# SwiGLU of an fp32 hybrid decoder: the second product of two token tiles in seven block products, its operands split and stored by the first product

## The chip, the cores and the metric

The kernel runs on one core of a Trainium2 chip. The metric is the device time of one execution in microseconds. Smaller is better.

## What is computed

One inference step of a decoder with two layers, on 1024 prompt tokens and 32 sample tokens (8 sequences of 4), with 1024 channels. Layer 0 mixes tokens by windowed attention, layer 1 by a gated linear recurrence, and each layer ends with the same gated feed-forward block, which is where most of the work lies:

```
def swiglu(h, w_in, w_out):
    g, u = jnp.split(h @ w_in, 2, axis=-1)
    return (jax.nn.silu(g) * u) @ w_out

for layer in range(DEPTH):                      # DEPTH = 2
    ...                                         # attention or recurrence
    xp = xp + swiglu(rms_norm(xp, ffn_norm[layer]), w_ffn_in[layer], w_ffn_out[layer])
    xs = xs + swiglu(rms_norm(xs, ffn_norm[layer]), w_ffn_in[layer], w_ffn_out[layer])
```

The hidden width is 2816, that is 22 blocks of 128, so `h @ w_in` is a product with 1024 x 5632 and the second one with 2816 x 1024. Everything is float32.

## The kernel before

**Data and precision.** Channels lie on the partitions, tokens along the free axis. The 1056 tokens are three tiles, t = 0 and 1 with 384 columns, t = 2 with 288 (256 prompt tokens and the 32 sample tokens). A float32 product is made from three matmuls in the faster fp32r format: every operand is split into a high part (a copy to fp32r, on ACT) and a low part (the value minus the high part, on DVE), and `mm3` (L244) issues high times high, high times low and low times high into one PSUM bank. So a block product of 128 x 128 with 384 columns is three matmuls on PE.

**Phases.** Attention lasts to about 390 us of the span, the first feed-forward block to about 1121, the recurrence to about 1458, the second feed-forward block to the end. Each feed-forward block (`ffn_phase`) has two halves.

**First product.** For each hidden block f, the gate and the up weights are loaded (`Weight`: one DMA of 512 KB, a copy on ACT, L83, a subtraction on DVE, L87). Blocks 0 and 1 are plain: `h_in` runs 48 matmuls for each tile. For f = 2 to 21 tiles 0 and 1 together are a 2 x 2 block problem (two tiles by two halves of the 1024 input channels, gate and up beside each other) that `seven` solves with seven block products in place of eight, in Strassen's manner: 84 matmuls of 384 columns, where the plain form has 96. The sums of inputs that it needs are formed once per layer (`sums`, `sum4`), those of weights once per f on DVE (`Sums`, L110 to L116). Tile 2 stays plain (48 matmuls of 288). Hidden values go to DRAM (`store`, L801, 192 KB for a block of 384 columns).

**Second product.** `outs` goes over 11 chunks of two hidden blocks each, and in a chunk over the three tiles. `Hidden` loads the stored values back and splits them (ACT L282, DVE L283). `h_out` takes, for each of the 8 output blocks m, one PSUM bank and 6 matmuls, and DVE adds the bank to the running x (L923). Per chunk that is 96 matmuls of 384 columns and 48 of 288. Nothing is waited for in a chunk but the DVE add eight banks back: there are 8 PSUM banks and each is used once.

**What sets the order.** PE and the DMA queue of SP run in the order in which the code issues. ACT, DVE and POOL are put in order by the scheduler of the language, at build time: the order of their instructions is fixed in the program, and each engine takes them strictly one after the other, so an instruction that waits holds all behind it. `drive` (L220) walks over the list of items; before an item runs, whatever it needs is prepared, and after it as many further preparations as slots are free for. There are 6 slots for split weights, 2 buffers `raw` for what has just been loaded, 18 slots of activations and 6 more ("h").

**Scores of the attention.** `att_rounds` computes the scores of a unit (four heads, 128 queries) from two halves of the partitions, 64 channels each. For each half one bank is taken, and for each of two heads one `mm3`: 6 matmuls of 64 partitions in the one half, then 6 in the other.

Of the kernel before, what the change touches and what calls it, by code (L numbers as in the profile page):

```python
# [29 lines left out]
NT = 3  # L30
# [25 lines left out]
class Slots:  # L56
    def __init__(self, names):
        self.free = list(names)
# [84 lines left out]


class Item:
    def __init__(self, fn, needs=(), frees=None):
        self.fn, self.needs = fn, list(needs)
        self.frees = self.needs if frees is None else list(frees)
        self.halves = [self]
# [36 lines left out]
class Kern:  # L186
# [33 lines left out]
    def drive(self, items):  # L220
        need = [w for it in items if isinstance(it, Item) for w in it.needs]
# [263 lines left out]
    def att_rounds(self, t):  # L485
# [5 lines left out]
        def scores(u):  # L491
# [8 lines left out]
            qc = slice(b * P, (b + 1) * P)  # L500
            jobs = []
            for hf in range(2):
                r = slice(hf * 64, hf * 64 + 64)
                ps = self.bank("s")
                for hh in range(2):
                    o = ps[:, hh * 256:hh * 256 + N]
                    self.mm3(o, q[r, hh, 0, qc], q[r, hh, 1, qc], kt[r, 0, k0:k0 + N], kt[r, 1, k0:k0 + N], True, True)
                    jobs.append((o, 8 * p + 4 * hf + 2 * hp + hh, hf * 2 + hh))
            st[u] = (jobs, nk, i, p, hp)
# [251 lines left out]
    def ffn_phase(self, l, before, after):  # L761
# [6 lines left out]
        hs = Slots([f"h{i}" for i in range(6)])  # L768
        T, HD_ = {}, {}
        late = []  # L770
        NPL = 2
        tt = nc.vector.tensor_tensor

        def enter():
# [4 lines left out]
            dp = pool("dF", space=bass.MemoryType.DRAM)  # L779
            for c in range(NF // 2):  # L780
                for t in range(NT):
                    HD_[c, t] = dp.tile([P, 2, WID[t]], F32, name=self.nm("hd"), tag=f"hd{c}_{t}")
            if l == 0:
# [16 lines left out]
        def store(f, t, src):  # L800
            late.append(lambda: nc.sync.dma_start(HD_[f // 2, t][:, f % 2, :], src))  # L801


        def h_in(wg, wu, f, t, mid=(), last=False):
# [9 lines left out]
            def post():  # L814
                sg = self.tmp([P, WMAX], "sg")
                nc.scalar.activation(sg[:, :W], g[:, :W], AF.Silu)  # L816
                tt(sg[:, :W], u[:, :W], sg[:, :W], OP.mult)  # L817
                store(f, t, sg[:, :W])

# [42 lines left out]
        def seven(wg, wu, ws, f):  # L862
            wc, wd = ws
            B11, B21, B22 = self.xn[0][:2], self.xn[0][2:], self.xn[1][2:]
            Tx = {i: [x[0] for x in T[i]] for i in T}

# [5 lines left out]

            A, B, C, Dk = self.bank(), self.bank(), self.bank(), self.bank()
            pc, u2 = small(f"e{2 * (f % 2)}"), small(f"e{2 * (f % 2) + 1}")
            prod(A, wg, 0, B11, True)
            nc.scalar.activation(pc, A[:, :WMAX], AF.Copy)
            prod(B, wd, 0, Tx[2], True)
            tt(u2, B[:, :WMAX], pc, OP.add)
            prod(C, wc, 0, Tx[3], True)
            tt(pc, C[:, :WMAX], u2, OP.add)  # L880
            prod(Dk, wc, 1, Tx[1], True)
            tt(pc, Dk[:, :WMAX], pc, OP.add)
            flush()
            prod(A, wg, 1, B21, False)
            sg = self.tmp([P, WMAX], "sg")
            nc.scalar.activation(sg, A[:, :WMAX], AF.Silu)
            prod(Dk, wd, 1, B22, False)
            g1 = self.gt.tile([P, WMAX], F32, name=self.nm("xs"), tag="xs", bufs=2)
            tt(g1, Dk[:, :WMAX], u2, OP.add)  # L889
            nc.scalar.activation(g1, g1, AF.Silu)  # L890
            prod(C, wu, 1, Tx[4], False)
            if f == NF - 1:
                self.freeall(self.xn[0] + self.xn[1][2:])
                for i in T:
                    for x, s in T[i]:
                        s.put(x[1])

            def post():
                tt(pc, pc, g1, OP.mult)
                store(f, 1, pc)  # L900
                tt(u2, C[:, :WMAX], u2, OP.add)
                tt(u2, u2, sg, OP.mult)
                store(f, 0, u2)

            return post


        def h_out(w0, w1, h, ch, t, fin, mid):
            W = WID[t]
            ws = (w0, w1)  # L910
            groups = [(m, 1) for m in range(KB)]
            if fin:
                groups = groups[4:] if l == 1 and t == 2 else [(4, 4)]
                groups = [(0, 4)] + groups
            for m0, grp in groups:
                pss = [self.bank() for _ in range(grp)]
                for c in range(2):
                    for ps, m in zip(pss, range(m0, m0 + grp)):
                        self.mm3(ps[:, :W], ws[c][:, 0, m * P:(m + 1) * P], ws[c][:, 1, m * P:(m + 1) * P],
                                 h[:, c, 0, :W], h[:, c, 1, :W], c == 0, c == 1)  # L920
                for ps, m in zip(pss, range(m0, m0 + grp)):
                    x = self.xview(t, m)
                    nc.vector.tensor_tensor(x, ps[:, :W], x, OP.add)  # L923
                    if fin and (l == 1 or t < 2):
                        self.square(t, m)
                if m0 + grp == 4:
                    for fn in mid:
                        fn()

# [12 lines left out]

        def outs(ch, fin=False, mid=((), (), ())):
            w = [Weight(I[f"wd{l}"][2 * ch + k], True) for k in range(2)]
            h = [Hidden(HD_, ch, t, hs, lambda: self.hp) for t in range(NT)]
            return [Item(lambda a, b, h, t=t: h_out(a, b, h, ch, t, fin, mid[t]), w + [h[t]],
                         (w if t == 2 else []) + [h[t]]) for t in range(NT)]

        n0, n1 = after
# [6 lines left out]
        for f in range(NPL, NF):  # L956
            L += blocks(f)
        L += [flush]
        nch = NF // 2
        for ch in range(nch - 2):  # L960
            if l == 0:
                L.append(lambda b=ch: self.caches(b) if b < DB else None)
            L += outs(ch)
        p = outs(nch - 2, False, ((), n0[1:2], n1[1:2]))
        o = outs(nch - 1, True, ((), n0[3:4], n1[3:4]))
        L += [p[0], o[0], p[1], o[1]] + n0[4:] + [p[2], o[2]] + n1[4:]
        if l == 0:
# [371 lines left out]
```

## Time and profile before

| what | value |
|---|---|
| median of three runs | 2211.83 us (2208.38 to 2214.43) |
| the profiled execution | 2209.49 us, its span 2207.7 us |
| mean granted TensorE clock | 0.994 of full speed |
| PE busy | 2167.9 us, 98% of the span |
| DVE / ACT / POOL busy | 1491.5 / 899.8 / 117.8 us |
| moved by DMA | 198.01 MB, mean 90 GB/s |

The profiled execution is 1.8 us longer than its span (what lies before the first and behind the last instruction that is counted), and 2.3 us below the median of the three runs. In the profile L12 means line 12 of the kernel; a row of a group gives the engine, the operation, out<-in by the names of the program, the shape and the count. Times are microseconds unless marked ns. PE is the matmul side of TensorE, PEld its loads of weights, DVE is VectorE, ACT is ScalarE, POOL is GpSimd.

### The profile page before, as it was taken

The numbers are of one execution on the slowest core, as the hardware profiler recorded it, in microseconds if no ns is written. First come the engines' busy times: TensorE is split into PE (matmuls) and PEld (weight loads), VectorE is DVE, ScalarE is ACT, GpSimd is POOL, SyncE is SP. The second block draws the span as 40 slices with busy tenths as digits, with TensorE's granted clock in tenths as the row PEclk, the third lists the DMA queues.
The fourth block names the chain that finished last, engine by engine and source line by source line (L and its number), as shares of the span: only waits on it lengthen the run. The fifth ranks groups of instructions, "written<-read, shape, count | busy, mean of one in ns | idle before, by whom it ended". The sixth has DMA issues, their size and how long they took to land.

```text
span 2207.7 us, 35068 instructions
## 1 busy us (share of the span) xinstructions
PE 2167.9 (98%) x13848; PEld 2145.6 (97%) x13848; DVE 1491.5 (68%) x2928; ACT 899.8 (41%) x1595; POOL 117.8 (5%) x168
## 2 busy tenths in 40 slices
PE   9999999999999999999999989999999999999997
PEld 8999999999999999999999989999999999999997
DVE  6776778855555556777786787788555555577766
ACT  5666665422223223211268887753222322321213
POOL 1223231000000000000000000000000000000002
PEclk9999999999999999999999999999999999999998
DMA  5332334212222124333212123421222212343222
GB/s 191 99 102 81 105 104 137 68 59 87 76 70 87 62 84 150 109 100 94 62 51 65 58 86 110 131 77 61 87 66 80 87 58 87 105 126 91 88 69 79
DMA packets 76045, 198.01 MB, mean 90 GB/s; under 512 B 9256, under 2 KB 32360, under 8 KB 75880
## 3 DMA queue, kind: packets, MB, share of 16 engines
q1 hardware_dynamic: 75120, 195.45, 27.7%
q8 instruction: 108, 1.77, 0.3%
q14 instruction: 57, 0.47, 0.1%
q10 hardware_dynamic: 760, 0.33, 0.1%
HBM read 167.12 MB, written 30.62 MB: 90 GB/s over the span
## 4 chain that ended last, share of the span: by engine, by line
PE 87%; DVE 7%; ACT 3%; issue 1%; DMA 1%; POOL 1%; SPq 0%; DVEq 0%; POOLq 0%; ACTq 0%
PE mm L244 82%; PE s L244 1%; DVE w L87 1%; PE pt L552 1%; DVE xs L349 1%; ACT w L83 1%; DVE xn L283 1%; DVE s L522 0%; DVE acc L300 0%; POOL x L1199 0%; DMA raw<-in_wg 0%; ACT g L1062 0%; DVE g L1110 0%; PE mm L307 0%; DVE T L283 0%
## 5 line engine op out<-in xcount | busy, mean ns | idle before, releaser
L244 PE MATMUL mm<-xn,w 128*128 128x384 f32 (+1 forms) x5808 | 929.0, 318 | 16.8 <-DVE x L687 4.6
L244 PEld LDWEIGHTS mm<-xn,w 128*128 128x128 f32 x5808 | 903.1, 189 | 23.4 <-issue 4.8
L244 PE MATMUL mm<-h,w 128*128 128x384 f32 (+1 forms) x3168 | 511.2, 322 | 1.0 <-DVE rc L311 0.6
L244 PEld LDWEIGHTS mm<-h,w 128*128 128x128 f32 x3168 | 508.8, 188 | 1.3 <-DVE rc L311 0.8
L83 ACT ACTIVATE w<-raw 128x1024 fp32r<-128x1024 f32 x248 | 262.0, 1058 | 394.8 <-PE mm L244 162.1
L87 DVE TENSOR_TENSOR w<-raw,w 128x1024 fp32r<-128x1024 f32 x246 | 300.8, 1224 | 100.4 <-ACT w L83 95.5
L244 PE MATMUL mm<-T,w 128*128 128x384 f32 x1920 | 350.9, 338 | 0.0
L923 DVE TENSOR_TENSOR x<-mm,x 128x384 f32<-128x384 f32 (+1 forms) x528 | 265.0, 521 | 116.9 <-PE mm L244 116.6
L244 PEld LDWEIGHTS mm<-T,w 128*128 128x128 f32 x1920 | 338.7, 188 | 0.0
L817 DVE TENSOR_TENSOR sg<-mm,sg 128x288 f32<-128x288 f32 (+1 forms) x52 | 24.5, 470 | 176.7 <-PE mm L244 176.6
L111 ACT ACTIVATE w<-raw 128x1024 fp32r<-128x1024 f32 x40 | 42.4, 1060 | 209.5 <-PE mm L244 207.6
L282 ACT ACTIVATE h<-raw 128x768 fp32r<-128x768 f32 (+1 forms) x66 | 52.1, 789 | 174.5 <-PE mm L244 141.8
L312 POOL TENSOR_TENSOR rc<-rc,mhalf 128x3 f32<-128x3 f32 x15 | 13.8, 923 | 1634.1 <-DVE rc L311 1628.9
L244 PE MATMUL mm<-att,w 128*128 128x384 f32 (+1 forms) x576 | 97.4, 325 | 0.3 <-DVE att L283 0.3
L544 POOL TENSOR_SCALAR s<-s,sm 128x256 f32<-128x256 f32 (+1 forms) x128 | 85.4, 686 | 208.9 <-DVE sm L542 85.6
L244 PEld LDWEIGHTS mm<-att,w 128*128 128x128 f32 x576 | 91.3, 188 | 2.5 <-DVE att L283 0.5
L244 PE MATMUL mm<-y,w 128*128 128x384 f32 (+1 forms) x576 | 93.6, 322 | 0.0
L244 PEld LDWEIGHTS mm<-y,w 128*128 128x128 f32 x576 | 92.4, 188 | 0.1
L816 ACT ACTIVATE sg<-mm 128x288 f32<-128x288 f32 (+1 forms) x52 | 22.0, 422 | 146.2 <-PE mm L244 146.0
L529 ACT ACTIVATE s<-s,sm 128x256 f32<-128x256 f32 (+1 forms) x128 | 61.7, 483 | 46.2 <-DVE sm L526 43.9
L283 DVE TENSOR_TENSOR h<-raw,h 128x768 fp32r<-128x768 f32 (+1 forms) x66 | 58.5, 886 | 15.5 <-ACT h L282 15.3
L889 DVE TENSOR_TENSOR xs<-mm,e 128x384 f32<-128x384 f32 x40 | 22.3, 558 | 66.9 <-PE mm L244 66.9
(192 smaller groups left out, 2010.9 us busy)
## 6 DMA issues: line engine op xcount, KB each, us to landing
raw<-in_wg SPq DMA_DIRECT2D x44, 512.0 KB, 3.7
raw<-in_wu SPq DMA_DIRECT2D x44, 512.0 KB, 4.4
raw<-in_wd SPq DMA_DIRECT2D x44, 512.0 KB, 3.6
raw<-hd SPq DMA_DIRECT2D x44, 384.0 KB, 3.1
hd<-e SPq DMA_DIRECT2D x80, 192.0 KB, 1.9
raw<-in_wq SPq DMA_DIRECT2D x24, 512.0 KB, 3.6
raw<-in_wo SPq DMA_DIRECT2D x24, 512.0 KB, 3.6
raw<-in_wxb SPq DMA_DIRECT2D x16, 512.0 KB, 3.6
```

What stands on the lines that cost most here:

```text
L83: nc.scalar.activation(self.t[:, 0, :], raw, AF.Copy)
L87: nc.vector.tensor_tensor(self.t[:, 1, :], raw, self.t[:, 0, :].bitcast(F32), OP.subtract)
L111: nc.scalar.activation(c[:, 0, :], u, AF.Copy)
L244: mm = lambda *a, **k: self.nc.tensor.matmul(*a, skip_group_check=more, **k)
L282: nc.scalar.activation(hi, src, AF.Copy)
L283: nc.vector.tensor_tensor(lo, src, hi.bitcast(F32), OP.subtract)
L349: nc.vector.scalar_tensor_tensor(y[:, :W], self.xview(t, kb), self.gcol(gname, kb), self.rs[t][:, :W], op0=OP.mult, op1=OP.mult)
L529: nc.scalar.activation(s[:, j, :N], s[:, j, :N], AF.Exp, bias=sm[:, 1, j:j + 1], accum_out=sm[:, 3, j:j + 1])
L544: nc.gpsimd.tensor_scalar(s[:, j, :N], s[:, j, :N], sm[:, 4, j:j + 1], 1.0, op0=OP.mult, op1=OP.mult)
L817: tt(sg[:, :W], u[:, :W], sg[:, :W], OP.mult)
L889: tt(g1, Dk[:, :WMAX], u2, OP.add)
L923: nc.vector.tensor_tensor(x, ps[:, :W], x, OP.add)
```

## The change

**The second product of f = 2 to 21.** The 20 hidden blocks make 5 chunks of 4, and a chunk has 4 units (mp = 0 to 3), each for two output blocks. For tiles 0 and 1 a unit is again a 2 x 2 problem (two pairs of hidden blocks by two output blocks) and runs seven products of 6 matmuls with 384 columns, 42 where the plain form has 48. In four chunks tile 2 stands in the middle of the unit (`plain`, two groups of 12 matmuls of 288); in the last chunk the 8 plain groups come after all units, with steps of the next norm between them. f = 0 and 1 stay plain (`outs`).

**Three banks in a unit.** The seven products need three PSUM banks: a product is added to x by DVE, and a later product is accumulated on top of the same bank and added to another block of x. So a later product waits for the DVE add of the earlier one.

**Sums of weights.** The four 128 x 256 blocks of a unit's weight (re-laid on the host as `wz`) are loaded as one `Weight`. `MixSums` then makes four sums in the loaded buffer on POOL, each from the one before (L159 to L162), and splits them (ACT L329, DVE L330) into a second weight slot.

**Operands from the first product.** The sums of hidden values that the seven products need (b11, b21, b22, t1 to t4) are formed at the end of each odd f (`keep_pair`), split there (`keep`: ACT L868, DVE L869) and stored as high and low part with two DMAs (L870, L871). `Operand` loads them back with one DMA each (2 x 2 x 384 columns, 786 KB) without work on ACT or DVE. Tile 2 is handled in the same way.

**`seven` in the first product** uses three banks in place of four: three intermediate products are copied out by ACT (L969, L971, L973), and PE waits for the copies before it uses the banks anew.

**Scores.** Two banks are taken at once, and the matmuls of the two partition halves alternate.

**Loads of caches** for the first 8 sequences are issued before the first 8 units of layer 0 instead of before the first 8 chunks.

The core of the diff:

```diff
+class MixSums:
+    def prep(self, k):
...
+        a, b, c, d = (r[:, i * 256:(i + 1) * 256] for i in range(4))
+        tt = nc.gpsimd.tensor_tensor
+        tt(d, c, d, OP.add)
+        tt(c, a, c, OP.subtract)
+        tt(a, d, a, OP.subtract)
+        tt(b, b, a, OP.subtract)
+        self.t = self.slot[0].tile([P, 2, 1024], F32R, name=k.nm("w"), tag=self.slot[1])
+        k.split(self.t[:, 0, :], self.t[:, 1, :], r)
...
     def att_rounds(self, t):
...
+            pss = [self.bank("s") for _ in range(2)]
+            for hh in range(2):
+                for a, c in ((0, 0), (1, 0), (0, 1)):
+                    for hf in range(2):
+                        r = slice(hf * 64, hf * 64 + 64)
+                        nc.tensor.matmul(pss[hf][:, hh * 256:hh * 256 + N], q[r, hh, a, qc], kt[r, c, k0:k0 + N],
+                                         start=a + c == 0, stop=c == 1)
...
+        def keep(dst, src):
+            W = src.shape[-1]
+            T["n"] = T.get("n", 0) + 1
+            hi = self.tmp([P, WMAX], "hi", bufs=1) if T["n"] % 2 else \
+                self.gt.tile([P, WMAX], F32, name=self.nm("hi"), tag="xs", bufs=2)
+            hi = hi[:, :W]
+            nc.scalar.activation(hi.bitcast(F32R), src, AF.Copy)
+            tt(src.bitcast(F32R), src, hi, OP.subtract)
+            nc.sync.dma_start(dst[:, 0, :], hi)
+            nc.sync.dma_start(dst[:, 1, :], src)
...
+            t1, b12 = T.pop("even")
+            t2, t4 = g("rs"), g("acc")
+            tt(t2, h1, t1, OP.subtract)
+            tt(b12, h1, b12, OP.subtract)
+            tt(t4, h0, t2, OP.subtract)
+            for i, x in zip(KEEP[1:], (h0, h1, t1, t2, b12, t4)):
+                keep(od(i), x)
...
         def seven(wg, wu, ws, f):
...
+            A, B, Dk = self.bank(), self.bank(), self.bank()
...
             prod(A, wg, 0, B11, True)
+            nc.scalar.activation(sg, A[:, :WMAX], AF.Copy)
+            prod(Dk, wc, 0, Tx[3], True)
+            nc.scalar.activation(p7, Dk[:, :WMAX], AF.Copy)
+            prod(A, wd, 0, Tx[2], False)
+            nc.scalar.activation(u2, A[:, :WMAX], AF.Copy)
+            prod(B, wg, 1, B21, True)
...
+        def unit(w, ws, o, mp, fin, hh=None):
+            b11, b21, b22, t1, t2, t3, t4 = o
+            m0, m1 = 2 * mp, 2 * mp + 1
...
+            A, B, Dk = self.bank(), self.bank(), self.bank()
+            prod(A, w, 0, b11, True)
+            add(0, m0, A)
+            prod(Dk, ws, 2, t3, True)
+            add(1, m1, Dk)
+            prod(B, w, 1, b21, True)
+            add(0, m0, B, fin)
+            prod(A, ws, 0, t2, False)
+            add(0, m1, A)
+            if hh:
+                plain(w, hh, m0, False)
+            prod(Dk, w, 3, t4, False)
+            add(0, m1, Dk, fin)
+            prod(A, ws, 3, t1, False)
+            add(1, m1, A, fin)
+            if hh:
+                plain(w, hh, m1, False)
+            else:
+                add(1, m0, A)
+                A = self.bank()
+            prod(A, ws, 1, b22, not hh)
+            add(1, m0, A, fin)
```

How the order of instructions moves is shown at three places. The first is PE in the second product of layer 0. Before, in the middle of a chunk, each bank `mm` gets three matmuls with each of the two weights of the chunk (two rows), and the next bank follows:

```order
L244 MATMUL mm_1208_9362<-h_1149_8990,w_1136_8910 128x384 x3
L244 MATMUL mm_1208_9362<-h_1149_8990,w_1138_8915 128x384 x3
L244 MATMUL mm_1209_9370<-h_1149_8990,w_1136_8910 128x384 x3
L244 MATMUL mm_1209_9370<-h_1149_8990,w_1138_8915 128x384 x3
L244 MATMUL mm_1210_9378<-h_1149_8990,w_1136_8910 128x384 x3
L244 MATMUL mm_1210_9378<-h_1149_8990,w_1138_8915 128x384 x3
```

Now, at the end of unit 6 and the start of unit 7 (w_1335 is the weight of unit 7 and w_1336 its sums, the `o` are the stored operands):

```order
L291 MATMUL mm_1353_10249<-o_1298_9696,w_1322_9972 128x288 x6
L291 MATMUL mm_1353_10249<-o_1299_9698,w_1322_9972 128x288 x6
L291 MATMUL mm_1349_10190<-o_1285_9592,w_1323_9979 128x384 x6
L291 MATMUL mm_1357_10284<-o_1283_9588,w_1335_10076 128x384 x6
L291 MATMUL mm_1359_10286<-o_1296_9692,w_1336_10083 128x384 x6
L291 MATMUL mm_1358_10285<-o_1284_9590,w_1335_10076 128x384 x6
L291 MATMUL mm_1357_10284<-o_1287_9596,w_1336_10083 128x384 x6
```

Unit 7 uses its sums in its second product already, and its first bank again in its fourth. The second place is DVE in the same stretch. Before, adds of banks (L923) stand in a row, and the low part of a weight (L87) stands between them, long before PE needs it:

```order
L923 TENSOR_TENSOR x_286_1987<-mm_1212_9394,x_286_1987 128x384
L923 TENSOR_TENSOR x_286_1987<-mm_1213_9402,x_286_1987 128x384
L87 TENSOR_TENSOR w_1207_9357<-raw_1206_9355,w_1207_9357 128x1024
L923 TENSOR_TENSOR x_286_1987<-mm_1214_9410,x_286_1987 128x384
L923 TENSOR_TENSOR x_286_1987<-mm_1215_9418,x_286_1987 128x384
L923 TENSOR_TENSOR x_472_3466<-mm_1218_9431,x_472_3466 128x384
```

Now, at the same border of units 6 and 7 (the first row is the last add of unit 6):

```order
L1001 TENSOR_TENSOR x_473_3467<-mm_1349_10190,x_473_3467 128x384
L87 TENSOR_TENSOR w_1335_10076<-raw_1334_10074,w_1335_10076 128x1024
L1001 TENSOR_TENSOR x_286_1987<-mm_1357_10284,x_286_1987 128x384
L330 TENSOR_TENSOR w_1336_10083<-raw_1334_10074,w_1336_10083 128x1024
L1001 TENSOR_TENSOR x_473_3467<-mm_1359_10286,x_473_3467 128x384
L1001 TENSOR_TENSOR x_286_1987<-mm_1358_10285,x_286_1987 128x384
L1001 TENSOR_TENSOR x_286_1987<-mm_1357_10284,x_286_1987 128x384
L1001 TENSOR_TENSOR x_628_4440<-mm_1360_10315,x_628_4440 128x288
```

Both steps of unit 7's weights stand at its own start. The third place is DVE in layer 1, at the start of unit 26, where the two steps belong to unit 28 (w_2710 its weight, w_2711 its sums):

```order
L1001 TENSOR_TENSOR x_472_3466<-mm_2704_20587,x_472_3466 128x384
L87 TENSOR_TENSOR w_2710_20669<-raw_2709_20667,w_2710_20669 128x1024
L1001 TENSOR_TENSOR x_286_1987<-mm_2712_20679,x_286_1987 128x384
L1001 TENSOR_TENSOR x_473_3467<-mm_2714_20681,x_473_3467 128x384
L1001 TENSOR_TENSOR x_286_1987<-mm_2713_20680,x_286_1987 128x384
L330 TENSOR_TENSOR w_2711_20676<-raw_2709_20667,w_2711_20676 128x1024
L1001 TENSOR_TENSOR x_286_1987<-mm_2712_20679,x_286_1987 128x384
```

Here the low part of the sums (L330) of a unit two further on stands ahead of the fourth add of unit 26. Over the whole program PE has 13,503 matmuls in place of 13,743: 240 of 128x384 fewer.

More of the change, by code (lines that the diff above doesn't have):

```diff
@@ L801, in store, with place, keep_pair @@
             late.append(lambda: nc.sync.dma_start(HD_[f // 2, t][:, f % 2, :], src))
+        def place(f):
+            return (f - NPL) // 4, (f - NPL) % 4 // 2, f % 2
+        def keep(dst, src):
[8 more added lines that the diff above has]
+            nc.sync.dma_start(dst[:, 1, :], src)
+        def keep_pair(f, h0, h1):
+            c, j, half = place(f)
+            g = lambda tag: self.gt.tile([P, WMAX], F32, name=self.nm("t"), tag=tag, bufs=2)
+            od = lambda i: OD[c, i][:, j]
+            if half == 0:
+                st1 = T["even"] = (g("acc"), h1)
+                tt(st1[0], h1, h0, OP.subtract)
+                keep(od("b11"), h0)
+                return
+            t1, b12 = T.pop("even")
[5 more added lines that the diff above has]
+                keep(od(i), x)
         def h_in(wg, wu, f, t, mid=(), last=False):
@@ L817, in post @@
                 tt(sg[:, :W], u[:, :W], sg[:, :W], OP.mult)
-                store(f, t, sg[:, :W])
+                if f < NPL:
+                    store(f, t, sg[:, :W])
+                else:
+                    c, j, half = place(f)
+                    keep(OD[c, j][:, half], sg[:, :W])
             return post
@@ L909, in h_out, with add @@
+            return post
+        def add(t, m, ps, fin=False):
+            x = self.xview(t, m)
+            tt(x, ps[:, :WID[t]], x, OP.add)
+            if fin:
+                self.square(t, m)
+        def h_out(w0, w1, h, t):
             W = WID[t]
             ws = (w0, w1)
[L911 to L916, printed above, removed]
-                for c in range(2):
[L918 to L928, printed above, removed]
@@ new lines, in h_out, with plain @@
+            for m in range(KB):
+                ps = self.bank()
+                for c in range(2):
+                    self.mm3(ps[:, :W], ws[c][:, 0, m * P:(m + 1) * P], ws[c][:, 1, m * P:(m + 1) * P],
+                             h[:, c, 0, :W], h[:, c, 1, :W], c == 0, c == 1)
+                add(t, m, ps)
+        def plain(w, hh, m, fin):
+            W = WID[2]
+            ps = self.bank()
+            for j in range(2):
+                for half in range(2):
+                    c = slice((m % 2 * 2 + half) * 256 + j * P, (m % 2 * 2 + half) * 256 + (j + 1) * P)
+                    self.mm3(ps[:, :W], w[:, 0, c], w[:, 1, c], hh[j][:, half, 0, :W], hh[j][:, half, 1, :W],
+                             j + half == 0, j + half == 2)
+            add(2, m, ps, fin and l == 1)
@@ L957, in ffn_phase @@
             L += blocks(f)
[L958 to L966, printed above, removed]
+        p = outs()
+        m, q = mixed()
+        m[0].ahead += m[0].needs[2:]
+        L += p
+        for i, x in enumerate(m):
+            if l == 0 and i < DB:
+                L.append(lambda b=i: self.caches(b))
+            L.append(x)
+        L += [q[0]] + n0[1:2] + [q[1]] + n0[3:] + [q[2]] + n1[1:2] + [q[3]] + n1[3:]
         if l == 0:
```

129 lines of the change are left out of this document (88 added, 41 removed).

## The prediction

> **What bounds the kernel now.** I read the page's busy times and its chain of waits first. The chain lists what released the work that ended last, as shares of the span:
>
> ```profile
> PE 2167.9 (98%) x13848; PEld 2145.6 (97%) x13848; DVE 1491.5 (68%) x2928; ACT 899.8 (41%) x1595; POOL 117.8 (5%) x168
> PE 87%; DVE 7%; ACT 3%; issue 1%; DMA 1%; POOL 1%; SPq 0%; DVEq 0%; POOLq 0%; ACTq 0%
> PE mm L244 82%; PE s L244 1%; DVE w L87 1%; PE pt L552 1%; DVE xs L349 1%; ACT w L83 1%; DVE xn L283 1%; DVE s L522 0%; DVE acc L300 0%; POOL x L1199 0%; DMA raw<-in_wg 0%; ACT g L1062 0%; DVE g L1110 0%; PE mm L307 0%; DVE T L283 0%
> ```
>
> PE bounds the kernel. Where it does so without a gap is told by busy time by stretch (length, then busy time and count for PE and PEld, DVE, ACT, POOL, the clock, DMA):
>
> ```profile
> 60.00:100.00 40.00, 38.38 (x266) 35.95 (x265) 31.43 (x98) 26.17 (x77) 9.21 (x17) 0.96 0.33 99
> 300.00:350.00 50.00, 49.38 (x361) 44.38 (x360) 41.08 (x130) 31.52 (x92) 15.16 (x22) 1.00 0.19 64
> 700.00:1100.00 400.00, 400.00 (x2491) 400.00 (x2490) 257.97 (x423) 96.60 (x124) 0.98 (x2) 1.00 0.31 95
> 1900.00:2160.00 260.00, 260.00 (x1618) 260.00 (x1617) 179.92 (x309) 57.11 (x72) 0.00 (x0) 1.00 0.31 95
> ```
>
> In the feed-forward blocks PE never pauses, so a matmul less there is its pitch less, and any wait put there is paid whole. The pitch comes from PE's timeline, where a run of 12 matmuls with 384 columns starts at 705.00 and the next run at 707.11:
>
> ```profile
> 705.00 2.27 PE L244 MATMUL mm<-T,w 128*128 128x384 f32 x12
> 707.11 0.30 PE L244 MATMUL mm<-xn,w 128*128 128x288 f32 x1
> ```
>
> That is 2.11 / 12 = 0.1755, about 0.175 us. The 2.27 us overlap their successors and are no pitch. Why the second product has no wait shows on DVE's timeline, which idles for PE between adds (the bracket is idle time and its releaser):
>
> ```profile
> 908.38 1.23 DVE L87 TENSOR_TENSOR w<-raw,w 128x1024 fp32r<-128x1024 f32 x1 [0.23 <-ACT w L83]
> 911.88 0.56 DVE L923 TENSOR_TENSOR x<-mm,x 128x384 f32<-128x384 f32 x1 [0.21 <-PE mm L244]
> 912.92 0.56 DVE L923 TENSOR_TENSOR x<-mm,x 128x384 f32<-128x384 f32 x1 [0.49 <-PE mm L244]
> ```
>
> DVE is the one that waits, and a late add costs nothing, because each of 8 banks is used in turn.
>
> **What is removed.** 240 matmuls of 128x384 at 0.175 us are 41.9 us, all in the stretches with PE at 100%: **-41.9**.
>
> **Scores.** One unit of scores, and what follows it on PE:
>
> ```profile
> 78.21 1.32 PE L244 MATMUL s<-kT,q 64*128 64x256 f32 x12
> 79.46 0.79 PE L244 MATMUL mm<-xn,w 128*128 128x384 f32 x3
> ...
> 78.56:78.67 0.11, 0.11 (x4) 1.00 0.00 0
> ```
>
> Twelve starts take 1.25 us. The last row is a stretch of 0.11 us of the scores alone: four of them are under way in it, so they already overlap. If six pairs start side by side at that pitch, with some 0.4 us for entering and leaving as now, a unit takes about 1.0 us: 0.25 less, and 0.35 less at the best. Times 32 units: 8 to 11 us. PE also waits for others in these stretches (38.38 of 40, 49.38 of 50), and the wait for the softmax stays. I take **-7**, between 0 and -11.
>
> **The waits in the second product.** This is the term that decides. By the pitch of 0.175 us for 384 columns (and 0.131 for 288, the same scaled), a unit in the first four chunks takes 42 x 0.175 + 24 x 0.131 = 10.5 us. Counted from its start, PE begins its second product, the first with the unit's sums, at 1.05, and the one that adds to the first bank a third time at 6.83; for this the fourth add must be done. DVE's fixed order puts the weights' two steps between those adds. How long the chain from the one step (L87) to the other (L330) takes follows from these rows of groups (minimum/median/maximum in ns, or busy time and mean):
>
> ```profile
> L87 DVE TENSOR_TENSOR w<-raw,w x246: 1195/1225/1347, 17.4 to 2119.8; 128x1024 fp32r<-128x1024 f32 x123
> L83 ACT ACTIVATE w<-raw x248: 1039/1061/1069, 5.1 to 2118.5; 128x1024 fp32r<-128x1024 f32 x124
> L544 POOL TENSOR_SCALAR s<-s,sm x128: 370/483/1895, 72.2 to 345.3; 128x256 f32<-128x256 f32 x112, 128x128 f32<-128x128 f32 x16
> L1199 POOL TENSOR_TENSOR x<-x,rs 128x384 f32<-128x384 f32 x8 | 8.6, 1111 | 5.2 <-ACT rs L332 5.2
> L1199 POOL TENSOR_TENSOR x<-x,rs 128x288 f32<-128x288 f32 x2 | 1.5, 794 | 2.2 <-ACT rs L332 2.2
> L218 POOL TENSOR_TENSOR w<-raw,w 128x512 fp32r<-128x512 f32 x4 | 5.6, 1436 | 4.1 <-ACT w L83 4.1
> ```
>
> POOL's sum of 128x256 is not in the trace. Two thirds of 1111 ns are 741, half of 1436 are 718, 794 scaled by 256/288 is 706: I take 0.75 us with its start. The nearest row of the same shape, with one tensor as input, has 483 ns: the lower bound. The upper bound is 1.0 us, nearly the whole row of 384, as DVE may hold POOL up: L544's maximum of 1895 ns shows that something does. The Trainium skill (GPSIMD Engine Reference, § 3.1) gives 4497 ns for a sum of two tensors with 2048 elements, in proportion 0.56 us for 256; the sum below would by that come to about -8 instead of +12. The rows of 288 and 384 lie above that proportion (0.63 and 0.84 us), so I stay with the rows.
>
> So in most units of layer 1 (the third place of the order): the add before ends at 0.76, L87 1.97, four sums 5.1, ACT's copy 6.2, L330 7.47, fourth add 8.0. PE wants it at 6.83: **1.2 us** of wait. Where the two steps stand one add later each, it is about 0.6. Behind the waiting L330 stand all later adds. In units 7 and 8 (the second place of the order) both steps are the unit's own: its sums are ready at 7.47 and wanted at 1.05, less 0.3 for what the unit before still overlaps: **6.1 us** each.
>
> I walked through DVE's order for all 40 units in this way. Layer 0: unit 0 3 (its weight also waits behind the last stores and the first loads on SP's queue), unit 4 5.1, units 7 and 8 12.2, unit 16 2.8 (the last chunk has no tile 2 between), unit 11 1.65, units 12 and 15 2.4, units 5, 9 and 14 1.8, units 17 and 18 0.8: **+29.8**. Layer 1: unit 20 3, unit 23 2.25, nine units of 1.2 10.8, unit 36 2.8, three of 0.6 1.8, two of 0.4 0.8: **+21.5**. If POOL's sum takes 0.1 us less, each wait that is left shrinks by 0.4, some 10 us in all; if the cover of POOL were perfect, the term would be near nothing.
>
> **The clock.** At the start of the first feed-forward block PE stands still for 4.64 us, and the clock of the stretch behind is halved:
>
> ```profile
> 389.50 6.43 PE L244 MATMUL mm<-xn,w 128*128 128x384 f32 x24 [4.64 <-DVE x L687]
> 387.00:394.00 7.00, 4.50 (x14) 4.53 (x15) 6.86 (x12) 4.12 (x7) 0.00 (x0) 0.51 0.58 159
> ```
>
> 7 us at 0.51 lose about 3.4 us of full speed. Three waits of 5 to 6 us are forecast (units 4, 7, 8), and the matmuls right behind one may fall into such a window in part: **+4**, between 0 and 3 x 3.4 = 10.
>
> **The first product.** Per odd f it gains six `keep`s: six ACT copies and subtractions of 384 columns and twelve stores on SP. ACT has 3.5 us of this in 42, and is busy for 96.6 us of the 400 from 700 to 1100. The stores:
>
> ```profile
> hd<-e SPq DMA_DIRECT2D x80, 192.0 KB, 1.9
> L801 SPq DMA_DIRECT2D hd<-e x80: 319/326/1210, 454.8 to 1934.7; - x80
> ```
>
> 12 issues of 0.33 are 4 us of SP's queue, with one weight behind. A `hi` buffer is free again about 0.5 (copy) + 0.55 + 0.65 + 1.9 = 3.6 us after it is taken, and three of them go round. PE's new waits for ACT's copies (L969 to L973) come at least one product of 2.1 us after the bank is written, the copy takes about 0.5 us, and whatever stands ahead of it on ACT leaves some 0.7 to 0.95 us: **+2**, cover by a hair. If it is gone, each odd f pays 1 to 2 us, 20 times.
>
> **The ends.** Between the phases and at the end the norms follow the last chunk, which has less to cover them; at the end POOL's eight sums (8.6 us above) now come after the small power that they had preceded: **+4** for both ends together, 0 to 8 (a part of those 8.6 us is all that can move).
>
> **The sum.** -41.9 - 7 + 29.8 + 21.5 + 4 + 2 + 4 = +12.4, from 2209.5 for the profiled execution: **2222 us**. The median of the runs shown is 2.3 us above that execution, well inside the range. About 0.3%, 6.6 us, is what a measurement of this kernel can tell from no change.
>
> **The rivals.**
>
> *A: POOL's sums are short, DVE's order then holds PE little.* With 0.48 us (the L544 row), the chain is 4 x 0.27 = 1.1 us shorter. The waits of 0.4 to 1.2 us are gone (about 17 us of the 51.3), and the nine larger ones lose 1.1 each (10): 51.3 becomes about 24. The sum is then -14, **2195 us**; without the clock's and the ends' share 2187. It decides from about 0.62 us per sum downwards: there the time is as before. Against it speaks that all three rows with two tensors lie above; for it, that none has this shape. Chance 0.27. The figure of the Trainium skill above would put the time into this rival. This is the side of faster.
>
> *B: the first product waits on its own stores.* If ACT's queue stands still for a `hi` buffer whose stores have not landed, L969 and L973 come late behind it, and PE waits 1 to 2 us in each of the 20 odd f: +20 to +40 on top, **2242 to 2262**, say 2250. For it: 0.7 us of slack against stores whose issue alone can take 1210 ns by the row. Against: DMA stands at a share of 0.31. Chance 0.14.
>
> *C: the alternating halves bring nothing,* as the pairs overlap already (four under way in 0.11 us): +7, **2229**. Chance 0.12.
>
> *The forecast:* 0.47, its own range 2208 to 2240.
>
> **How the numbers follow.** Faster by over 0.3% (below 2205): nearly all of A, 0.23, and 0.02 of the forecast's edge: 0.25. Within 0.3%: 0.04 of A, 0.08 of the forecast, 0.02 of C: 0.14. Slower: 0.37, 0.10 and B's 0.14: 0.61. The range reaches into A down to 2186 and into B up to 2252; beyond lie A with no wait left at all (0.08) and the upper part of B (0.08).
>
> **What would show it.** Right: on the profile after, PE idles in the second product for DVE's adds (L1001) and for the sums' low parts (L330), about 25 us per layer, with single waits of 5 to 6 us at units 4, 7 and 8; POOL's sums (L159 to L162) at 0.7 to 0.8 us; the chain of waits names POOL, ACT and DVE there; a unit of scores at 1.0 us. Wrong: POOL's sums below 0.6 us or above 1, PE busy at 100% between L87 and L330, waits for ACT's L969 to L973 in the first product, or the scores at 1.25 us as before.

## The result and the profile after

The changed kernel takes 2239.87 us (median of 4 runs, 2238.54 to 2241.23), the kernel before 2212.11 us beside it (4 runs). The ratio is 1.0127, 95% interval 1.011 to 1.0145: 28 us slower, where 10 to 12 were forecast. The profiled execution has a span of 2239.0 us against 2207.7, 31.3 us more. The page's busy times and chain now:

```profile
PE 2145.5 (96%) x13608; PEld 2109.3 (94%) x13608; DVE 1514.5 (68%) x2976; ACT 1010.8 (45%) x1835; POOL 242.8 (11%) x328
PE 75%; DVE 11%; ACT 5%; POOL 5%; issue 2%; DMA 2%; SPq 0%; POOLq 0%; ACTq 0%; DVEq 0%
```

PE has 240 matmuls less (13608 against 13848 in the profile), but its busy time fell by 22 us only, not by 42, and POOL, which was not on the chain before with more than 1%, holds 5% of it. Busy time by stretch tells where the time went. The stretches are the second product of layer 0, all between, and the second product of layer 1, first of the kernel before (length, then busy time and count of PE, PEld, DVE, ACT, POOL, then clock, DMA share, GB/s):

```profile
861.20:1121.58 260.38, 258.22 (x1611) 257.38 (x1610) 191.41 (x349) 57.25 (x77) 2.10 (x3) 1.00 0.31 93
1121.58:1932.77 811.19, 800.28 (x4994) 797.37 (x4992) 540.40 (x1026) 403.64 (x631) 4.09 (x5) 1.00 0.26 82
1932.77:2191.23 258.46, 257.48 (x1610) 257.01 (x1608) 188.43 (x345) 57.56 (x83) 3.76 (x5) 1.00 0.28 86
```

and of the changed kernel:

```profile
859.14:1140.38 281.24, 251.34 (x1484) 243.88 (x1482) 166.24 (x283) 56.03 (x68) 63.32 (x81) 0.95 0.46 172
1140.38:1955.50 815.12, 804.32 (x4999) 801.50 (x5000) 578.49 (x1118) 459.39 (x759) 6.54 (x8) 0.99 0.33 108
1955.50:2220.11 264.61, 244.67 (x1484) 239.58 (x1482) 163.43 (x281) 59.98 (x76) 64.27 (x82) 0.98 0.46 173
```

Up to the first of these stretches the changed kernel is 2.06 us ahead (859.14 against 861.20). Then it loses 20.86 us in the second product of layer 0, 3.93 between, 6.15 in that of layer 1, and 2.4 behind it (2239.0 - 2220.11 against 2207.7 - 2191.23): together 31.3. Each second product has 127 or 126 matmuls less, of which 120 are the ones taken out; the others are small ones that now come behind it.

In the second products PE idles for 29.9 and 19.9 us (length less busy time), against 2.2 and 1.0 before. Who ended these waits, first in layer 0, then in layer 1 (total us, times, longest):

```profile
PE mm L291 <- DVE x L1001: 15.9, 12, 3.5
PE mm L291 <- ACT w L329: 10.0, 3, 3.3
PE mm L291 <- DVE w L87: 3.1, 3, 1.4
PE mm L291 <- DVE w L330: 0.8, 3, 0.3
...
PE mm L291 <- DVE x L1001: 19.9, 16, 3.6
```

The timeline shows both kinds that the prediction spoke of. Layer 1, a unit whose DVE queue holds the low part of the sums of the unit two further on (L87, POOL's four sums, ACT's copy, L330, then the adds):

```profile
2101.11 1.22 DVE L87 TENSOR_TENSOR w<-raw,w 128x1024 fp32r<-128x1024 f32 x1
2102.41 0.73 POOL L159 TENSOR_TENSOR raw<-raw 128x256 f32<-128x256 f32 x1 [6.83 <-DVE w L87]
2104.86 0.74 POOL L162 TENSOR_TENSOR raw<-raw 128x256 f32<-128x256 f32 x1
2105.63 1.06 ACT L329 ACTIVATE w<-raw 128x1024 fp32r<-128x1024 f32 x1 [5.58 <-POOL raw L162]
2106.72 1.23 DVE L330 TENSOR_TENSOR w<-raw,w 128x1024 fp32r<-128x1024 f32 x1 [2.36 <-ACT w L329]
2107.86 1.38 DVE L1001 TENSOR_TENSOR x<-mm,x 128x384 f32<-128x384 f32 x3
2108.47 10.82 PE L291 MATMUL mm<-o,w 128*128 128x384 f32 x66 [1.02 <-DVE x L1001]
```

DVE waits 2.36 us for ACT, three adds stand behind L330, and PE pays 1.02 us. Layer 0, unit 7, whose own two steps stand at its start:

```profile
970.18 1.22 DVE L87 TENSOR_TENSOR w<-raw,w 128x1024 fp32r<-128x1024 f32 x1
971.46 0.98 PE L291 MATMUL mm<-o,w 128*128 128x384 f32 x4 [1.43 <-DVE w L87]
974.66 1.06 ACT L329 ACTIVATE w<-raw 128x1024 fp32r<-128x1024 f32 x1 [18.47 <-POOL raw L162]
975.76 1.01 PE L291 MATMUL mm<-o,w 128*128 128x384 f32 x2 [3.33 <-ACT w L329]
```

1.43 and 3.33 us, 4.8 in all. What the prediction priced too low is what follows such waits. In consecutive stretches of 3.41 us, the grid on which the granted clock changes:

```profile
889.45:892.86 3.41, 2.28 (x17) 2.04 (x15) 0.46 (x1) 1.06 (x1) 3.10 (x6) 1.00 1.02 419
892.86:896.28 3.42, 1.07 (x6) 1.07 (x7) 2.30 (x4) 1.00 (x1) 2.31 (x2) 1.00 1.01 420
896.28:899.69 3.41, 3.41 (x13) 3.41 (x12) 2.62 (x4) 0.60 (x2) 0.00 (x0) 0.50 1.04 432
```

In the first PE idles for 1.13 us and nothing follows; in the second it idles for 2.35 us, and the third runs at 0.50: 13 matmuls where 20 would go. This is one wait of 3.48 us for an add. Where a wait falls on the grid matters too: one of 2.78 us in the same layer, which ends at 1041.11, lies over two stretches with 1.31 and 1.47 us idle, and no half-clock stretch follows. In the clock's record the second product of layer 0 has five half-clock stretches, 27.3 us in sum with PE busy for 21.9 of them, that of layer 1 three, 10.2 us, PE busy throughout. Half of the busy part is lost: 11.0 and 5.1 us.

### The profile page after: what moved, and what is told of

Same layout as the page of the kernel before. It is cut to its first block, busy times and chain, and to the rows that moved or that the text cites. A ratio compares the mean times of both kernels' runs of the same rounds, so it can differ in the third digit from the quotient of the medians.

```text
span 2239.0 us, 35153 instructions
## 1 busy us (share of the span) xinstructions
PE 2145.5 (96%) x13608; PEld 2109.3 (94%) x13608; DVE 1514.5 (68%) x2976; ACT 1010.8 (45%) x1835; POOL 242.8 (11%) x328
## 4 chain that ended last, share of the span: by engine, by line
PE 75%; DVE 11%; ACT 5%; POOL 5%; issue 2%; DMA 2%; SPq 0%; POOLq 0%; ACTq 0%; DVEq 0%
PE mm L291 71%; DVE w L87 3%; DVE x L1001 2%; ACT w L329 1%; DVE w L330 1%; POOL raw L160 1%; ACT w L83 1%; POOL raw L161 1%; POOL raw L159 1%; POOL raw L162 1%; PE pt L602 1%; PE s L554 1%; DMA raw<-in_wq 1%; DVE s L572 1%; ACT s L579 1%
## 5 line engine op out<-in xcount | busy, mean ns | idle before, releaser
L291 PE MATMUL mm<-o,w 128*128 128x384 f32 (+1 forms) x2640 | 447.4, 330 | 49.8 <-DVE x L1001 35.8
L291 PEld LDWEIGHTS mm<-o,w 128*128 128x128 f32 x2640 | 434.0, 193 | 61.9 <-DVE x L1001 44.5
L87 DVE TENSOR_TENSOR w<-raw,w 128x1024 fp32r<-128x1024 f32 x246 | 299.4, 1223 | 123.6 <-ACT w L83 121.8
L83 ACT ACTIVATE w<-raw 128x1024 fp32r<-128x1024 f32 x248 | 261.5, 1056 | 223.1 <-PE mm L291 128.4
L1001 DVE TENSOR_TENSOR x<-mm,x 128x384 f32<-128x384 f32 (+1 forms) x416 | 211.9, 531 | 119.4 <-PE mm L291 118.4
L159 POOL TENSOR_TENSOR raw<-raw 128x256 f32<-128x256 f32 x40 | 30.6, 764 | 1264.9 <-DVE w L87 810.2
L329 ACT ACTIVATE w<-raw 128x1024 fp32r<-128x1024 f32 x40 | 42.4, 1060 | 259.1 <-POOL raw L162 259.1
L330 DVE TENSOR_TENSOR w<-raw,w 128x1024 fp32r<-128x1024 f32 x40 | 49.9, 1248 | 88.8 <-ACT w L329 88.8
L868 ACT ACTIVATE hi<-e 128x384 fp32r<-128x384 f32 x80 | 41.8, 523 | 84.2 <-DVE e L992 28.5
L346 ACT ACTIVATE sq<-x 128x384 f32<-128x384 f32 (+1 forms) x105 | 51.0, 491 | 59.4 <-DVE x L1001 38.8
L116 DVE TENSOR_TENSOR w<-raw,w 128x1024 fp32r<-128x1024 f32 x40 | 48.9, 1223 | 35.5 <-ACT w L114 35.4
L976 ACT ACTIVATE sg<-sg 128x384 f32<-128x384 f32 x40 | 21.0, 525 | 91.4 <-DVE sg L975 91.4
```

What stands on the lines that cost most here:

```text
L83: nc.scalar.activation(self.t[:, 0, :], raw, AF.Copy)
L87: nc.vector.tensor_tensor(self.t[:, 1, :], raw, self.t[:, 0, :].bitcast(F32), OP.subtract)
L116: tt(d[:, 1, :], g, d[:, 0, :].bitcast(F32), OP.subtract)
L159: tt(d, c, d, OP.add)
L291: mm = lambda *a, **k: self.nc.tensor.matmul(*a, skip_group_check=more, **k)
L329: nc.scalar.activation(hi, src, AF.Copy)
```

## The experiments

The runs were made on several chips, so each is compared with the kernel before that ran beside it, and two runs by their ratios to it (the changed kernel's is 1.0127). Two theories were set against each other. Theory one, the prediction's: DVE's fixed order holds the adds behind a low part of the sums that waits for POOL and ACT, and PE waits for the adds; half-clock stretches follow the longer waits. The rival: three banks used over and over make PE wait for the adds whatever stands between them.

**The scores alone.** Only the hunk in `att_rounds` is put into the kernel before:

```diff
-                    self.mm3(o, q[r, hh, 0, qc], q[r, hh, 1, qc], kt[r, 0, k0:k0 + N], kt[r, 1, k0:k0 + N], True, True)
+                    for hf in range(2):
+                        r = slice(hf * 64, hf * 64 + 64)
+                        nc.tensor.matmul(pss[hf][:, hh * 256:hh * 256 + N], q[r, hh, a, qc], kt[r, c, k0:k0 + N],
+                                         start=a + c == 0, stop=c == 1)
```

> The kernel before with the alternating scores and nothing else. The start of the first feed-forward block moved from 389.5 to 386.7 us in the changed kernel. If the scores alone did that, this run comes out 2 to 4 us below the kernel before (about 2209 against 2212), with a unit of scores near 1.0 us in place of 1.25 us. Rival: the pairs overlapped already, and nothing moves.

2204.78 us (11 runs) against 2207.99, ratio 0.9984 (0.9975 to 0.9992): 3 us, as expected. A unit of scores on PE's timeline of this run:

```profile
76.65 0.99 PE L507 MATMUL s<-kT,q 64*128 64x256 f32 x12
77.57 2.35 PE L244 MATMUL mm<-xn,w 128*128 128x384 f32 x12
```

It takes 0.92 us in place of 1.25. Times 32 that is 10.6 us if all units gain alike, more than was forecast, and 3 arrive. Who takes a part of the rest is seen in PE's waits for the split softmax values, before the values are multiplied in. They are 4.8 us in 6 places in this run (L283); the same row of the changed kernel is

```profile
PE mm L291 <- DVE pr L330: 5.3, 7, 1.1
```

and this the kernel before:

```profile
PE mm L244 <- DVE pr L283: 0.7, 2, 0.4
```

PE reaches that point sooner, and DVE is no faster: 4.1 us of this run's gain are waited away in this one row, 4.6 us in the changed kernel. Where the other 3 us go stays open.

**Without POOL's sums.** The four sums are left out, so the products with the second weight slot are made with the plain weights:

```diff
-        tt(d, c, d, OP.add)
-        tt(c, a, c, OP.subtract)
-        tt(a, d, a, OP.subtract)
-        tt(b, b, a, OP.subtract)
```

> The changed kernel without POOL's four sums per unit: the second weight slot is split straight from the loaded weight, so the products with it are left without their sums. Theory one (the fixed order on DVE holds the adds behind a low part that waits for POOL): the chain between L87 and L330 loses 3.1 us, PE's idle time in the second products falls from 50 us to 10 to 20, most half-clock windows there go, and the time is 2180 to 2200 us. Rival (three banks used over again make PE wait for the adds whatever stands between): the idle time stays at 40 us or more, and the time above 2230.

2190.87 us, ratio to before 0.9921 (0.9906 to 0.9936). The two second products:

```profile
857.44:1104.58 247.14, 239.14 (x1484) 235.07 (x1482) 165.72 (x283) 54.88 (x67) 1.03 (x2) 1.00 0.52 196
1922.72:2170.77 248.05, 240.58 (x1484) 234.67 (x1482) 163.17 (x281) 58.24 (x75) 2.10 (x3) 1.00 0.49 184
```

Idle time is 8.0 and 7.5 us, and the clock stays at 1.00. With the same three banks and the same adds, 34 us of waits are gone: the rival falls, and POOL's chain is shown to be the cause. The transfers are not: DMA is as busy here as in the changed kernel (a share of 0.52 and 0.49 against 0.46). In this run the low part of the second slot also follows right behind L87 in layer 1's order on DVE, so the chain became shorter and its place moved with it; the place alone is tried below.

**The sums on DVE.** One word is changed:

```diff
-        tt = nc.gpsimd.tensor_tensor
+        tt = nc.vector.tensor_tensor
```

> The changed kernel with the four sums on DVE in place of POOL. Theory one: DVE's order then holds no wait for another engine but ACT's copy, the sums stand between adds, and PE's idle time in the second products falls to 10 to 25 us: 2185 to 2210 us. Rival (the banks are reused too early, DVE has too little room): 1.6 us more of work per unit on DVE make the adds later still, and the time is 2240 or more.

2197.38 us, ratio 0.9951 (0.9937 to 0.9964): by the ratios some 39 us less than the changed kernel, with 1.7 us more of work on DVE in each unit. The second products:

```profile
857.44:1117.86 260.42, 244.43 (x1484) 239.86 (x1482) 192.88 (x360) 56.19 (x68) 1.03 (x2) 0.97 0.49 185
1935.00:2176.82 241.82, 238.02 (x1484) 236.92 (x1482) 187.97 (x358) 60.10 (x76) 2.10 (x3) 0.99 0.51 189
```

Layer 1 idles for 3.8 us; layer 0 still for 16.0 and at a clock of 0.97, since some units there have their own steps at their start, and chain and sums lie in a row (PE waits up to 2.6 us for ACT's L329 there).

**One edge of order.** The low part of the sums is traced at the end of a unit and put behind the seventh add:

```diff
-        k.split(self.t[:, 0, :], self.t[:, 1, :], r)
+        nc.scalar.activation(self.t[:, 0, :], r, AF.Copy)
+        k.lows.append((self.t, r))
...
+            with self.tc.issue_after(after.ins):
+                self.nc.vector.tensor_tensor(t[:, 1, :], r, t[:, 0, :].bitcast(F32), OP.subtract)
```

> The changed kernel with one edge of order per unit: the low part of the sums stands behind the seventh add of the unit during which it is made. Nothing else is taken away. Theory one: the waits of about 1.0 us for the fourth add go (some 13 of them, 10 of these in layer 1), those of units 4, 7 and 8 stay, as do most half-clock windows: 2220 to 2228 us. Rival (the place of this instruction does not matter, the banks do): 2240 as before.

2215.08 us, ratio 1.0035 (1.0021 to 1.0049): by the ratios some 20 us less than the changed kernel. That is a little more than expected: 2220 to 2228 us was 8 to 16 above a kernel before of 2212, and it is 7 above the one beside it. The second products of both layers, and the waits of layer 1:

```profile
857.76:1132.33 274.57, 249.79 (x1484) 243.48 (x1482) 166.77 (x282) 56.01 (x68) 62.41 (x81) 0.95 0.47 176
1949.39:2197.68 248.29, 239.50 (x1484) 238.07 (x1482) 165.03 (x280) 59.97 (x76) 63.84 (x82) 0.99 0.49 184
...
PE mm L299 <- DVE x L1009: 7.6, 3, 3.2
```

In layer 1 POOL's work is the same 63.8 us, and the wait for the adds fell from 19.9 us in 16 places to 7.6 in 3: there the place of one instruction on DVE decides, at the same speed of POOL. Layer 0 still idles for 24.8 us, with the waits of units 4, 7 and 8 left, as expected.

**The cache copies moved.** Layer 0 differs from layer 1 by the copies of caches between its first eight units. They are put between the blocks of the first product:

```diff
         for f in range(NPL, NF):
+            if l == 0 and f - NPL < DB:
+                L.append(lambda b=f - NPL: self.caches(b))
             L += blocks(f)
...
-            if l == 0 and i < DB:
-                L.append(lambda b=i: self.caches(b))
```

> The changed kernel with one thing moved: the 16 copies of caches from DRAM to DRAM are issued before the first eight odd and even blocks of the first product of layer 0 instead of before the first eight units. DVE's order of layer 0 then reads like that of layer 1: no unit has its own weight's low part at its start from unit 4 on. Theory one (DVE's fixed order, and the scheduler puts the weights late because it reckons these copies slow): the waits at units 4, 7 and 8 (14 us) and their half-clock windows (about 8 us) go, while some more of the waits of 1.0 us come in; the second product of layer 0 takes 262 to 268 us as that of layer 1 does, in place of 281, and the time is 2220 to 2228 us. Rival (the weights themselves arrive late there, by DMA): the waits stay, 2238 to 2242.

2224.14 us, ratio 1.007 (1.0055 to 1.0085), as expected. Layer 0's second product and its waits:

```profile
859.62:1123.43 263.81, 243.74 (x1484) 238.07 (x1482) 165.88 (x283) 57.15 (x68) 63.11 (x81) 0.99 0.48 176
...
PE mm L291 <- DVE x L1001: 20.1, 18, 3.2
```

263.8 us, as in layer 1, and no wait for ACT's L329 or for L87 is left. The copies themselves cost little (two issues on SP's queue); they only moved the weights' steps to a later place in DVE's order. That the weights came late by DMA, the rival, is ruled out by the changed kernel's own trace as well: ACT's last copy of a weight (L83) ahead of L87 of unit 7 starts at 955.14, and DVE takes up L87 at 970.18 without having idled for it. That the scheduler does so because it reckons the copies slow is argued, not shown.

**The order mended, POOL keeps the sums.** The edge and the moved copies from above, and two units' weights ahead of the next operands:

```diff
-        need = [w for it in items if isinstance(it, Item) for w in it.needs + it.ahead]
+        its = [it for it in items if isinstance(it, Item)]
+        need = [w for a, b in zip(its, its[1:] + [Item(None)]) for w in a.needs[:2] + b.needs[:2] + a.needs[2:] + a.ahead]
```

> The changed kernel with its order mended and no work moved between engines: copies of caches early, a unit's two weights prepared ahead of the next operands, and the low part of the sums behind the seventh add. POOL still makes the sums. Theory one: PE's idle time in each second product falls below 8 us, the half-clock windows there go, each takes 240 to 248 us, and the time is 2172 to 2186 us. Rival (the seven products need more banks or DVE time): idle time stays above 15 us in one of them and the time above 2200.

2189.23 us, ratio 0.991 (0.9895 to 0.9925), 3 us above the upper end that was expected. The two second products:

```profile
857.12:1103.82 246.70, 240.14 (x1484) 237.91 (x1482) 168.19 (x287) 57.61 (x69) 59.76 (x79) 0.99 0.53 196
1922.13:2168.62 246.49, 238.81 (x1484) 236.77 (x1482) 166.14 (x286) 60.60 (x78) 60.44 (x80) 0.99 0.51 193
```

The idle time is 6.6 us in layer 0 and 7.7 in layer 1, as expected; one wait of more than 3 us in the second unit of each layer was left (3.41 and 3.15), and the clock went to half behind it, which was not expected.

**The order mended, the sums on DVE.** The same without the edge, with the sums on DVE.

```diff
-        tt = nc.gpsimd.tensor_tensor
+        tt = nc.vector.tensor_tensor
```

> As the run with the order mended, but the sums on DVE in place of POOL and the low part where the scheduler puts it. Theory one: four sums of 0.415 us stand between the adds and take 1.7 us of DVE per unit, which has the room: 2172 to 2188 us, within 5 us of the version with POOL. Rival (DVE becomes the bound): above 2195.

2176.69 us, ratio 0.9849 (0.9833 to 0.9866), 12.5 us below the version with POOL, not within 5. All three stretches:

```profile
857.67:1097.52 239.85, 237.00 (x1484) 235.24 (x1482) 189.66 (x362) 57.10 (x68) 1.03 (x2) 1.00 0.54 201
1097.52:1915.05 817.53, 805.84 (x4999) 802.43 (x5000) 575.84 (x1117) 458.83 (x759) 5.20 (x6) 0.99 0.32 105
1915.05:2155.97 240.92, 236.99 (x1484) 235.27 (x1482) 188.26 (x363) 60.32 (x76) 2.10 (x3) 1.00 0.52 198
```

Now the second products are 20.5 and 17.5 us shorter than before, nearly the 21 us each that the removed matmuls are worth, with 2.9 and 3.9 us idle.

**Waits of known length.** Into the kernel before go 20 waits of PE, each behind copies in a row on ACT (five more copies in one run, one more in the other):

```diff
+                if t == 0 and m0 == 0 and not fin:
+                    y = self.tmp([P, WMAX], "sg")
+                    nc.scalar.activation(y, pss[0][:, :WMAX], AF.Copy)
+                    for _ in range(5):
+                        nc.scalar.activation(y, y, AF.Copy)
+                    pz = self.bank()
+                    nc.tensor.matmul(pz[:, 0:1], y[:, 0:P], self.ones[:, 0:1], start=True, stop=True)
```

> The kernel before with 20 added waits of PE, ten in each second product (one per chunk): six copies in a row on ACT from a bank, then a small matmul that reads the result. Each wait should be some 3.3 us. If a wait costs its length and the drain of PE's pipeline, about 0.16 us, the time is 2211 + 20 x 3.5 = 2280 us. If the clock is halved for the 3.41 us window after a window in which PE was idle for half, 1.7 us more come with each: about 2310 to 2315 us, with some 20 half-clock windows in the record.

One run, 2341.11 us. The waits, and the two second products:

```profile
PE mm L927 <- ACT sg L925: 72.8, 20, 5.5
...
861.52:1184.93 323.41, 285.06 (x1631) 281.02 (x1630) 194.85 (x349) 86.79 (x136) 2.09 (x3) 0.92 0.24 75
2000.24:2322.86 322.62, 285.06 (x1630) 281.39 (x1628) 192.20 (x345) 87.56 (x143) 3.76 (x5) 0.92 0.21 69
```

The second products grew by 63.0 and 64.2 us: 127.2 us for 72.8 us of waits, 6.4 us for a wait of 3.6. The clock is 0.92 there. That is more than was expected with the clock counted (5.2), since 12 of the 20 waits bring two half-clock stretches, not one, when PE idles in the first of the two as well.

> The kernel before with the same 20 added waits of PE, each of two copies on ACT in place of six, so about 1.3 us long. If what a wait costs beyond its length comes from half-clock windows, and a window must find PE idle for half of 3.41 us, no such window appears in the second products and each wait costs about its length and 0.2 us: 20 x 1.5 = 30 us, 2238 to 2246 us, against 6.4 us for each wait of 3.4 us before. If the cost goes with the length alone (6.4 / 3.4 = 1.9 of it), it is 20 x 2.4 = 48 us, about 2258 us.

One run, 2257.86 us. The waits and the second products:

```profile
PE mm L927 <- ACT sg L925: 26.9, 20, 2.4
...
861.37:1143.24 281.87, 266.39 (x1631) 262.34 (x1630) 194.31 (x349) 66.08 (x96) 2.09 (x3) 0.99 0.29 86
1959.03:2239.57 280.54, 266.01 (x1630) 262.34 (x1628) 191.46 (x345) 66.83 (x103) 3.76 (x5) 0.99 0.25 79
```

43.6 us for 26.9 us of waits, 2.2 for a wait of 1.35: more than expected. The clock record has four half-clock stretches here (behind the first wait of each layer, 2.1 and 2.4 us, and behind one of 1.57 in each), worth 6.8 us; in 16 of 20 places nothing of the kind follows. Some 0.5 us for each wait remain, in which the added matmul and its weight load are contained. So the total lies where "the length alone" had it, but the clock stayed at 0.99: in these two runs the cost beyond the length and the clock is 0.3 to 0.5 us for a wait, and the clock's part, 2.4 us for a wait of 3.6, hardly touches those of 1.2.

**The ends.** On top of the mended order with the sums on DVE:

```diff
-        L += [q[0]] + n0[1:2] + [q[1]] + n0[3:] + [q[2]] + n1[1:2] + [q[3]] + n1[3:]
+        L += [q[0]] + n0[1:2] + [q[1]] + n1[1:2] + n0[3:] + [q[2]] + n1[3:] + [q[3]]
```

> The version with the order mended and the sums on DVE, with the last steps put in another order: tile 1's sum of squares right after the second plain part and its spreading after the third, so that the last plain part and its successor cover the chain over DVE and POOL. Between the two second products 817.5 us are taken where the kernel before takes 811.2, with one half-clock window of 6.83 us behind waits of 2.12 and 1.27 us at the border to the recurrence. If these waits are the cause, the border loses them and the window: 811 to 813 us there, the end 16 to 18 us in place of 19.5, and 2167 to 2172 us in all. Rival: the time there is lost elsewhere, and the total stays at 2176.

2168.28 us, ratio 0.9807 (0.9794 to 0.9821). Between the second products:

```profile
1099.93:1910.63 810.70, 801.25 (x4993) 797.50 (x4992) 576.13 (x1115) 458.10 (x758) 4.09 (x5) 1.00 0.33 106
```

810.7 us in place of 817.5. About 2 of these 6.8 us only changed places, since the stretch before it now holds seven small matmuls more and takes 242.0 us in place of 239.9; some 4.7 are gained, and the end falls from 19.5 to 16.9 us (2175.5 - 2155.97 and 2168.6 - 2151.71). The border is mended, and this version beats both kernels: 42 us below the kernel before, 1.9%.

## Why the prediction was right in its direction and wrong in its size

It said slower for the reason that the runs showed, but 12.4 us where the profiled execution lost 31.3; the median lies at the upper edge of the forecast's own range, 2208 to 2240. Point by point:

- **What is removed, -41.9.** Right: in the version with the order mended, the second products are 38 us shorter with a few us of waits left. (2.11 / 12 is 0.1758, not 0.1755, which would make it 42.2.)
- **The waits, +29.8 and +21.5.** Right, a little high: 27.7 and 19.0 us more of idle time (29.90 - 2.16 and 19.94 - 0.98), 4.6 us less than forecast. The waits of 1.2 us were 1.02, those of unit 7 4.8 where 6.1 were reckoned. POOL's sums took 0.74 to 0.84 us in the mean, where 0.75 was assumed:

```profile
L161 POOL TENSOR_TENSOR raw<-raw 128x256 f32<-128x256 f32 x40 | 33.8, 844 | 3.1
L162 POOL TENSOR_TENSOR raw<-raw 128x256 f32<-128x256 f32 x40 | 29.5, 738 | 3.1
```

  The estimate of 0.56 us from the page of the Trainium skill (GPSIMD Engine Reference, § 3.1) was too low here, and rival A fell with it.
- **The clock, +4.** This is the step that failed. The prediction counted three waits of 5 to 6 us (units 4, 7 and 8) as those that halve the clock, by the one example of 4.64 us, and took the matmuls behind them to be hit in part. In truth the clock was halved behind 8 waits or groups of waits in the two second products, 16.1 us in place of 4. Behind units 4, 7 and 8, whose waits came in pieces of at most 3.34 us, PE's busy time at half speed was 15.3 us, which costs 7.6. The other five stretches follow waits of 2.60 to 3.58 us, which the prediction had not counted, and cost 8.5.
- **The cost of a wait beyond its length** was not in the sum at all. With the clock's part taken off, PE's busy time in the second products (251.3 - 11.0 and 244.7 - 5.1) is still 3.0 us each above what the removed matmuls leave (258.2 - 20.95 and 257.5 - 20.95): 6.1 us over the 37 waits of the rows above, 0.16 each. The added waits of known length show such a part as well (0.3 to 0.5 with the added matmul). That it is the end of the last matmul, which nothing overlaps, is argued.
- **The scores, -7.** The unit became shorter than forecast (0.91 us), the gain smaller: the first feed-forward block starts 2.75 us sooner (386.75 against 389.50), of which 0.7 are lost again in its first product. So the term is 4.3 too large. The prediction named the wait for the softmax and did not price it.
- **The first product, +2.** Right in kind, a loss of 0.7 us in layer 0; rival B fell. PE waited for ACT's copies for 0.8 us in all.
- **The ends, +4.** 3.9 us between the second products, with the first product of layer 1 in them, and 2.4 at the end: about right, and the order of the last steps is the reason, as the last run shows: with it changed, both get shorter.

By these, 12.4 + 12.1 (clock) + 6.1 (each wait's end) + 4.3 (scores) - 4.6 (waits) + 1.0 (first products and ends, 7.0 where 6 were reckoned) = 31.3.

## What to carry to other kernels

Where a product is accumulated on a bank that was read a moment ago, the vector engine's queue can lie on the critical path, and an instruction in it that waits for a chain over other engines is then paid by TensorE. Two remedies worked here, and both together gained more than either. By the ratios to the kernel before, one edge of order took some 20 us off the changed kernel and all three changes of order some 48; the sums on DVE alone, with their shorter chain, took some 39, and with two of the changes of order 61. A wait of TensorE has to be priced with what follows it: here 20 waits of 3.6 us cost 1.75 times their length, and waits of 2.6 us and more halved the clock in 8 of 9 cases of the changed kernel (one that was spread evenly over two stretches of the grid did not), while those around 1 us by themselves brought no half-clock stretch. An unrelated transfer in the program can move the order of a scheduled engine, so the order is to be looked at for each layer, not for one.

## What the runs showed of the hardware

The granted clock changes on a fixed grid of 3.413 us. In the feed-forward parts of all these traces a stretch of the grid at full speed with 1.2 us or less of PE idle was never followed by one at half speed, one with 1.81 us or more always was, and between the two both occur: 1.22 us (from 2154.87 in the mended order with the sums on DVE) was followed by one, 1.80 us (from 2006.34 in the run with the copies moved) was not. PE need not be idle for a whole stretch. Idle time is not all that counts, though: in the attention a stretch with 0.55 us idle was followed by one at half speed (from 311.58 in the run without POOL's sums). The Trainium skill (TensorE: Matmul & The Clock Gate, section "What's actually happening") has the free-running window of 3413 ns, with which the trace agrees, and one idle window as the condition for half speed; here 1.81 of 3.41 us idle was enough. In a stretch that runs at half speed already, less was enough for another: in the run with the long waits, 1.39 us of idle in the second row below is followed by a further stretch at 0.50, and so is 0.24 us later in the same run (from 2152.63). It is no threshold for all parts: in the recurrence of the kernel before, 0.50 us was not (from 1312.10).

```profile
1009.17:1012.58 3.41, 1.38 (x9) 1.06 (x7) 2.84 (x5) 3.31 (x6) 0.00 (x0) 1.00 0.02 5
1012.58:1016.00 3.42, 2.03 (x7) 2.03 (x8) 0.01 (x1) 2.26 (x4) 0.00 (x0) 0.50 0.93 296
1016.00:1019.41 3.41, 3.41 (x13) 3.41 (x12) 2.25 (x3) 0.07 (x1) 0.00 (x0) 0.50 0.13 46
```
